# Two of four weight-block sums of a Strassen pair: VectorE adds replaced by accumulating transfers

## The chip, the cores and the metric

The kernel runs on one core of one Trainium2 chip. The metric is the device time of one execution in microseconds (us): 1936.63 us, the median of three runs (1934.05 to 1936.67).

## The reference

A decoder of two layers over 512 tokens with 16 meta tokens in front (528 rows of width 1024, float32). Each layer has a SwiGLU feed-forward block, a token mixer (gated linear attention in layer 0, sliding-window attention in layer 1) and a second feed-forward block, each between two RMS norms. The change touches only the first product of the four feed-forward blocks:

```python
def swiglu(x, w_in, w_out):                       # D_MODEL 1024, D_FF 2816
    gate, up = jnp.split(x @ w_in, 2, axis=-1)
    return (jax.nn.silu(gate) * up) @ w_out
...
    h = h + 0.5 * rmsnorm(swiglu(rmsnorm(h, g[0]), w_ffn_in[layer, 0], w_ffn_out[layer, 0]), g[1])
```

## The kernel before, in words

**Precision.** A float32 operand is split into a high part in TensorE's fast float32 format and the rest. A product is three matmuls: high by high, low by high, high by low. Every weight block therefore passes from a raw tile (128x512, 256 KB, loaded by SP) through one copy on ScalarE (ACT, the high part) and one subtraction on VectorE (DVE, the rest) into a `w` tile of two halves.

**The feed-forward block.** The 22 hidden tiles are worked in four chunks, `FF_CHUNKS`. The first chunk (4 tiles) uses plain products. The other three chunks have six hidden tiles each. For each hidden tile the gate block g and the up block u are taken together as one 2x2 block matrix of weights and multiplied with the halves of the activations by a Strassen scheme: seven half-size products instead of eight. That makes 72 such pairs in the kernel (4 blocks, 3 chunks, 6 pairs). After each chunk, `out_steps` multiplies the hidden tiles with `w_out` (tiles named `y`).

**One pair.** The left operands of the seven products are named in `split_pair`: with r11 and r12 the two halves of g, and r21 and r22 the two halves of u, they are 11, 12 and 22 (as loaded) and the sums s1 = r21 + r22, s3 = r11 + r21, s2 = s3 + r22 and s4 = r12 + s2. `Strassen.head` does product 11, `body` does s1, s2, 12 and s3, and `tail` does s4 and 22. The order on TensorE (PE) is 11 of the next pair, s4 and 22 of this pair, then s1, s2, 12, s3 of the next, and so on. Each product is 12 matmuls over 264 columns (256 in layer 1). Seven products are one turn. Between products ACT copies results out of PSUM, because the banks are reused: `t.v` (line 778, after s1), `t.u2` (line 780, after s2), the copy into `d` (line 773, after 11). Product s3 adds onto the bank that the `t.u2` copy reads, so it waits for line 780. The hidden tile is split by lines 802 to 807.

**Order and queues.** The order of the work is planned at build time by `Flow`, a clock that counts PE time; jobs yield the time they expect to pass (2.2 us after a load, `STEP` between parts). Each engine then runs its own queue strictly in order. `part` (lines 245 and 246) is the ACT copy and the DVE subtraction of one block of a pair; line 251 is `add`; lines 226 and 227 do the same for plain units such as `w_out`. `raw_tile` takes the raw tiles in rotation from `RAWS` buffers; the SP load into a buffer waits until the buffer's last reader is done. `CHAINS = 2` pairs may be in splitting at once, and `RING = 10` limits the split blocks that wait for PE. GpSimd (POOL) has no work in these chunks; its own work is sums of squares and norms at the ends of the blocks.

In the trace, tiles of 11, 12 and 22 are named `w`, those of the four sums `w_s`, the bank for s4 of a chunk's last pair `e`, and the raw tiles `raw`.

Of the kernel before, what the change touches and what calls it, by code (L numbers as in the profile page):

```python
# [13 lines left out]
ALU = mybir.AluOpType  # L14
# [15 lines left out]
L1 = [(16, 256), (272, 256)]  # L30
L1W = [(16, 512)]
SLOTS = 32
RAWS = 8
RING = 10
STEP = 1.1
CHAINS = 2

CHAIN = 5
# [85 lines left out]
def trunk_kernel(ctx: ExitStack, tc, a, out):  # L124
    nc = tc.nc
    pe, act, dve, pool, sp = nc.tensor, nc.scalar, nc.vector, nc.gpsimd, nc.sync
    flow = Flow()

    cp = ctx.enter_context(tc.tile_pool(name="cp", bufs=1))
    rp = ctx.enter_context(tc.tile_pool(name="rp", bufs=RAWS))  # L130
    hp = ctx.enter_context(tc.tile_pool(name="hp", bufs=SLOTS))
# [15 lines left out]
    def pair_tile(name, dt=F32R):  # L147
        return hp.tile([P, 2, TOK], dt, tag="pair", name=name)
# [29 lines left out]
    units = []  # L178
# [35 lines left out]
    def slot(i):  # L214

        while live[0] + sum(n for j, n in owed.items() if j < i) >= limit[0]:
            yield room[0]
        live[0] += 1
        owed[i] -= 1

    def raw_tile(name):
        return rp.tile([P, 512], F32, tag="raw", name=name)
# [7 lines left out]
    def split_unit(i, raws):  # L230
        yield 2.2
        for raw, m in raws:
            yield from slot(i)
            split_part(i, raw, m)

    def split_pair(i, raws):


        r11, r12, r21, r22 = raws
        parts, ready = loaded[i]  # L240

        def part(name, src):
            yield from slot(i)
            w = pair_tile(f"w{i}_{name}")
            act.activation(w[:, 0, :512], src, AF.Copy)  # L245
            dve.tensor_tensor(w[:, 1, :512], src, w[:, 0, :512].bitcast(F32), op=ALU.subtract)  # L246
            parts[name].append(w)
            ready[name].finish(flow)

        def add(dst, src):  # L250
            dve.tensor_tensor(dst, dst, src, op=ALU.add)  # L251

        yield 2.2
        yield from part("11", r11)
        add(r11, r21)
        add(r21, r22)
        yield STEP
        yield from part("s1", r21)
        yield STEP
        yield from part("s3", r11)  # L260
        add(r11, r22)
        yield STEP
        yield from part("s2", r11)
        yield STEP
        yield from part("12", r12)
        add(r12, r11)
        yield STEP
        yield from part("s4", r12)
        yield STEP
        yield from part("22", r22)  # L270
        chains[0] -= 1
        prefetch()

    def load_unit():
        i = len(loaded)
        asked[0] += costs[i]
        owed[i] = costs[i]
        if isinstance(units[i], list):
            g, u = units[i]
            chains[0] += 1  # L280
            raws = [raw_tile(f"raw{i}_{k}") for k in range(4)]
            for k in (2, 0, 1, 3):
                sp.dma_start(raws[k], (g, u)[k // 2][:, k % 2 * 512 : (k % 2 + 1) * 512])
                dma_end[0] = max(dma_end[0], flow.clock) + 512 * 1.5e-3
            names = ("11", "12", "22", "s1", "s2", "s3", "s4")
            loaded.append(({k: [] for k in names}, {k: Job(None) for k in names}))
            gen = split_pair(i, raws)
        else:
            n = units[i].shape[-1]
            raws = []  # L290
            for c in range(0, n, 512):
                m = min(512, n - c)
                raws.append((raw_tile(f"raw{i}_{c}"), m))
                sp.dma_start(raws[-1][0][:, :m], units[i][:, c : c + m])
            dma_end[0] = max(dma_end[0], flow.clock) + n * 1.5e-3
            loaded.append([])
            gen = split_unit(i, raws)
        split_jobs.append(flow.spawn(gen, dma_end[0] - flow.clock))

    def prefetch():  # L300
        while len(loaded) < cap[0] and asked[0] + costs[len(loaded)] <= freed[0] + ahead[0]:
            if isinstance(units[len(loaded)], list) and chains[0] == CHAINS:
                break
            load_unit()
# [945 lines left out]
    raws = [[raw_tile(f"raw{i}_{c}") for c in (0, 512)] for i in range(2)]  # L1250
# [17 lines left out]
    x.rjob[0] = flow.spawn(factors(0), 2.0)  # L1268
    dma_end[0] = 1.0
    load_unit()  # L1270
    load_unit()
    load_h(1, 0, 2, 4, 6)
    flow.spawn(second(), SECOND)
# [120 lines left out]
```

## Time and profile before

| what | value |
|---|---|
| median of three runs | 1936.63 us (1934.05 to 1936.67) |
| profiled execution, first to last instruction (span) | 1931.9 us; 4.7 us less than the median run, which has the start and the end around it |
| mean granted TensorE clock | 0.993 |
| busy: PE, weight loads (PEld), DVE, ACT, POOL | 98%, 93%, 74%, 52%, 11% |
| instructions on POOL | 417 |
| loads of `raw` from `w_in` | 352 of 256 KB, median 2.9 us from issue to landing |
| hardware DMA queue | 172.11 MB, 28.5% of the 16 DMA engines |

An engine that is busy for 98% of the span leaves little to gain by relieving others; where it does wait, the chain of waits and the timeline name the engine it waited for. The busy shares are averages over stages, so the twelve chunks are read by themselves in the prediction. The start-to-start distance of neighbouring products on PE shows lost time better than the busy column, because matmuls overlap.

### The profile page before, as it was taken

The numbers are of one execution on the slowest core, as the hardware profiler recorded it, in microseconds if no ns is written. First come the engines' busy times: TensorE is split into PE (matmuls) and PEld (weight loads), VectorE is DVE, ScalarE is ACT, GpSimd is POOL, SyncE is SP. The second block draws the span as 40 slices with busy tenths as digits, with TensorE's granted clock in tenths as the row PEclk, the third lists the DMA queues.
The fourth block names the chain that finished last, engine by engine and source line by source line (L and its number), as shares of the span: only waits on it lengthen the run. The fifth ranks groups of instructions, "written<-read, shape, count | busy, mean of one in ns | idle before, by whom it ended". The sixth has DMA issues, their size and how long they took to land.

```text
span 1931.9 us, 37400 instructions
## 1 busy us (share of the span) xinstructions
PE 1893.9 (98%) x14522; PEld 1803.6 (93%) x14522; DVE 1420.2 (74%) x2868; ACT 1000.5 (52%) x2268; POOL 217.3 (11%) x417
## 2 busy tenths in 40 slices
PE   8999999999999999999999999999998999999997
PEld 8999999999999999999999898989976898989897
DVE  7885858676364788585887786868688779858584
ACT  5662636653245556363674553536645665636363
POOL 2000000311111300000033000000351140000002
PEclk9999999999999999999999999999998999999998
DMA  4332323322113123233351223333321212333331
GB/s 163 109 97 90 104 89 113 107 77 73 38 56 110 56 76 101 93 100 98 101 168 45 66 86 112 91 112 104 122 66 34 74 48 72 97 103 108 102 112 44
DMA packets 102145, 174.63 MB, mean 90 GB/s; under 512 B 11472, under 2 KB 24272, under 8 KB 101968
## 3 DMA queue, kind: packets, MB, share of 16 engines
q1 hardware_dynamic: 101680, 172.11, 28.5%
q8 instruction: 114, 1.87, 0.4%
q14 instruction: 63, 0.52, 0.1%
q10 hardware_dynamic: 288, 0.13, 0.0%
HBM read 170.10 MB, written 2.10 MB: 89 GB/s over the span
## 4 chain that ended last, share of the span: by engine, by line
PE 70%; DVE 19%; ACT 6%; issue 3%; POOL 1%; DMA 0%; SPq 0%; DVEq 0%; ACTq 0%; POOLq 0%
PE y L162 30%; PE x L162 16%; PE a L162 11%; DVE raw L251 5%; PE c L162 4%; DVE w_s L246 4%; DVE w L246 3%; ACT w_s L245 3%; PE d L162 2%; DVE w L227 1%; PE o L162 1%; ACT w L226 1%; PE sc L162 1%; PE po L162 1%; DVE hidl0f L807 1%
## 5 line engine op out<-in xcount | busy, mean ns | idle before, releaser
L246 DVE TENSOR_TENSOR w_s<-raw,w_s 128x512 fp32r<-128x512 f32 x288 | 194.1, 691 | 129.5 <-ACT w_s L245 127.2
L162 PE MATMUL y<-hidl0f,w 128*128 128x272 f32 (+1 forms) x2112 | 261.0, 285 | 0.0
L227 DVE TENSOR_TENSOR w<-raw,w 128x512 fp32r<-128x512 f32 x378 | 243.8, 672 | 20.7 <-ACT w L226 18.8
L162 PEld LDWEIGHTS y<-hidl0f,w 128*128 128x128 f32 x2112 | 258.9, 188 | 0.2
L245 ACT ACTIVATE w_s<-raw 128x512 fp32r<-128x512 f32 x288 | 175.3, 628 | 149.5 <-DVE raw L251 146.0
L162 PE MATMUL y<-hidl1f,w 128*128 128x512 f32 (+1 forms) x1344 | 249.4, 346 | 0.0
L162 PEld LDWEIGHTS y<-hidl1f,w 128*128 128x128 f32 x1344 | 212.3, 188 | 33.2 <-ACT hidl1f L407 0.3
L226 ACT ACTIVATE w<-raw 128x512 fp32r<-128x512 f32 x378 | 208.6, 587 | 33.9 <-PE y L162 29.2
L403 POOL TENSOR_TENSOR acc_post<-acc_post,sq_post 128x256 f32<-128x256 f32 (+1 forms) x72 | 59.1, 821 | 1383.3 <-ACT sq_post L402 1382.6
L251 DVE TENSOR_TENSOR raw<-raw,raw 128x512 f32<-128x512 f32 x288 | 198.0, 688 | 5.5
L246 DVE TENSOR_TENSOR w<-raw,w 128x512 fp32r<-128x512 f32 x216 | 148.4, 688 | 40.4 <-ACT w L245 39.1
L245 ACT ACTIVATE w<-raw 128x512 fp32r<-128x512 f32 x216 | 133.9, 621 | 47.9 <-PE y L162 47.6
L162 PE MATMUL x<-x_l0m,w 128*128 128x272 f32 (+1 forms) x1200 | 158.4, 289 | 0.0
L162 PEld LDWEIGHTS x<-x_l0m,w 128*128 128x128 f32 x1200 | 149.5, 189 | 1.1
L587 DVE TENSOR_TENSOR Y<-y,Y 128x256 f32<-128x256 f32 (+2 forms) x176 | 82.4, 473 | 73.5 <-PE y L162 73.0
L162 PE MATMUL a<-zl0f_t,w_s 128*128 128x264 f32 x864 | 117.6, 285 | 3.9 <-ACT c L780 3.9
L162 PE MATMUL a<-zl1f_t,w_s 128*128 128x256 f32 x864 | 115.3, 283 | 1.9 <-ACT c L780 1.6
L162 PEld LDWEIGHTS a<-zl0f_t,w_s 128*128 128x128 f32 x864 | 110.0, 188 | 5.2 <-ACT c L780 5.2
L162 PEld LDWEIGHTS a<-zl1f_t,w_s 128*128 128x128 f32 x864 | 107.0, 189 | 4.6 <-ACT c L780 4.5
L162 PE MATMUL x<-x_l0f,w 128*128 128x256 f32 (+1 forms) x768 | 100.8, 292 | 6.1 <-ACT w L226 5.7
L162 PEld LDWEIGHTS x<-x_l0f,w 128*128 128x128 f32 x768 | 97.5, 193 | 7.3 <-ACT w L226 5.9
L162 PE MATMUL x<-x_l1f,w 128*128 128x256 f32 (+1 forms) x576 | 92.8, 320 | 0.0
(485 smaller groups left out, 3318.8 us busy)
## 6 DMA issues: line engine op xcount, KB each, us to landing
raw<-in_w_in SPq DMA_DIRECT2D x352, 256.0 KB, 2.9
raw<-in_w_out SPq DMA_DIRECT2D x96, 256.0 KB, 3.3
raw<-in_gla_in SPq DMA_DIRECT2D x50, 256.0 KB, 3.1
raw<-in_w_last SPq DMA_DIRECT2D x48, 256.0 KB, 3.0
raw<-in_w_out SPq DMA_DIRECT2D x64, 128.0 KB, 2.9
raw<-in_gla_out SPq DMA_DIRECT2D x16, 256.0 KB, 2.8
raw<-in_w_q SPq DMA_DIRECT2D x16, 256.0 KB, 3.6
raw<-in_swa_out SPq DMA_DIRECT2D x16, 256.0 KB, 2.8
```

The costliest lines, as they stand in the source:

```text
L162: inst = pe.matmul(o, lhs, rhs, start=start, stop=stop, skip_group_check=onto)
L226: act.activation(w[:, 0, :m], raw[:, :m], AF.Copy)
L227: dve.tensor_tensor(w[:, 1, :m], raw[:, :m], w[:, 0, :m].bitcast(F32), op=ALU.subtract)
L245: act.activation(w[:, 0, :512], src, AF.Copy)
L246: dve.tensor_tensor(w[:, 1, :512], src, w[:, 0, :512].bitcast(F32), op=ALU.subtract)
L251: dve.tensor_tensor(dst, dst, src, op=ALU.add)
L403: pool.tensor_tensor(sums[0][:, :n], sums[0][:, :n], t[:, :n], op=ALU.add)
L587: dve.tensor_tensor(y, p[:, :n], y, op=ALU.add)
L807: dve.scalar_tensor_tensor(t.hid[:, 1, g], t.h, -1.0, t.hid[:, 0, g].bitcast(F32), op0=ALU.mult, op1=ALU.subtract)
```

## The change

Per pair, five raw tiles are loaded instead of four: r11, r12, r22, and two tiles that become sums, `r1` (loaded with the first half of u) and `r3` (loaded with the first half of g). POOL then issues two transfers from memory that add onto these tiles: the second half of u onto `r1`, which makes s1, and the first half of u onto `r3`, which makes s3. The two other sums stay on DVE: r22 onto `r3` (s2) and s2 onto r12 (s4). The planner's waits change: 2.2 us to the accumulating transfers (`LANDED`, as before), then 11, then 2.5 us (`ADDED`) before s1, and s3 comes one step after s1 as before. There are 11 raw buffers instead of 8, and the scratch for descriptors of POOL's transfers is set to 8192 bytes.

```diff
-RAWS = 8
+RAWS = 11
...
+LANDED = 2.2
+ADDED = 2.5
...
-        r11, r12, r21, r22 = raws
+        r11, r12, r22, r1, r3 = raws
         parts, ready = loaded[i]
+        (g, u), half = units[i], lambda t, c: t[:, c * 512 : (c + 1) * 512]
...
-        def add(dst, src):
-            dve.tensor_tensor(dst, dst, src, op=ALU.add)
-
-        yield 2.2
+        def onto(dst, src):
+            pool.dma_start(dst, src, accum_op=ALU.add)
+
+        yield LANDED
+        onto(r1, half(u, 1))
+        onto(r3, half(u, 0))
         yield from part("11", r11)
-        add(r11, r21)
-        add(r21, r22)
+        yield ADDED
+        yield from part("s1", r1)
         yield STEP
-        yield from part("s1", r21)
+        yield from part("s3", r3)
+        dve.tensor_tensor(r3, r3, r22, op=ALU.add)
         yield STEP
-        yield from part("s3", r11)
-        add(r11, r22)
-        yield STEP
-        yield from part("s2", r11)
+        yield from part("s2", r3)
         yield STEP
         yield from part("12", r12)
-        add(r12, r11)
+        dve.tensor_tensor(r12, r12, r3, op=ALU.add)
...
-            raws = [raw_tile(f"raw{i}_{k}") for k in range(4)]
-            for k in (2, 0, 1, 3):
-                sp.dma_start(raws[k], (g, u)[k // 2][:, k % 2 * 512 : (k % 2 + 1) * 512])
+            raws = [raw_tile(f"raw{i}_{k}") for k in range(5)]
+            for k, src, c in ((0, g, 0), (3, u, 0), (4, g, 0), (2, u, 1), (1, g, 1)):
+                sp.dma_start(raws[k], src[:, c * 512 : (c + 1) * 512])
...
-    nc = bacc.Bacc("TRN2", target_bir_lowering=False, num_devices=1)
+    nc = bacc.Bacc("TRN2", target_bir_lowering=False, num_devices=1, dynamic_dma_scratch_size=8192)
```

Line numbers of the changed kernel are 2 or 3 higher: 778, 780, 782 and 806 become 781, 783, 785 and 809. On DVE 144 additions go, on POOL 144 transfers come (two for each pair, with nothing between those of a chunk), on SP 72 loads come. Outside the twelve chunks the order on PE, ACT and DVE stays as it was, apart from a few matmuls of one `w_out` product.

**PE at the end of the first chunk.** Before: product 12 of the last pair (tile `d`), five matmuls of s4 (`e`), then s3 (`a_1`), then the rest of s4.

```order
L162 MATMUL d_1136<-zl0f_211_946,w_12_1780 128x264 x6
L162 MATMUL e_1897<-zl0f_220_766,w_s_1801 128x264 x5
L162 MATMUL a_1_1133<-zl0f_t_1000,w_s_1735 128x264 x6
L162 MATMUL a_1_1133<-zl0f_t_1017,w_s_1735 128x264 x6
L162 MATMUL e_1897<-zl0f_220_766,w_s_1801 128x264
L162 MATMUL e_1897<-zl0f_221_781,w_s_1801 128x264 x6
```

The same place now:

```order
L164 MATMUL d_1140<-zl0f_210_923,w_12_1815 128x264 x6
L164 MATMUL d_1140<-zl0f_211_945,w_12_1815 128x264 x6
L164 MATMUL a_1_1137<-zl0f_t_1002,w_s_1771 128x264 x6
L164 MATMUL a_1_1137<-zl0f_t_1019,w_s_1771 128x264 x6
L164 MATMUL e_1909<-zl0f_220_766,w_s_1842 128x264 x6
L164 MATMUL e_1909<-zl0f_221_781,w_s_1842 128x264 x6
```

The five matmuls of s4 that stood ahead of s3 now stand behind it.

**ACT at the same place.** From the copy into `d` (after product 11 of the last pair) to the `t.u2` copy (line 780, now 783), which s3 waits for. Before:

```order
L773 ACTIVATE d_1136<-a_1_1133 128x264
L245 ACTIVATE w_s_1757<-raw_0_1606 128x512
L226 ACTIVATE w_1_1777<-raw_512_1651 128x256
L245 ACTIVATE w_12_1780<-raw_1_1607 128x512
L226 ACTIVATE w_0_1798<-raw_0_1689 128x512
L795 ACTIVATE c_1616<-c_1616 128x264
L245 ACTIVATE w_s_1801<-raw_1_1607 128x512
L226 ACTIVATE w_1_1820<-raw_512_1691 128x256
L245 ACTIVATE w_22_1825<-raw_3_1609 128x512
L806 ACTIVATE hidl0f_8_1615<-c_1616 128x528
L778 ACTIVATE c_1750<-c_1_1135 128x264
L226 ACTIVATE w_0_1843<-raw_0_1727 128x512
```

Now:

```order
L776 ACTIVATE d_1140<-a_1_1137 128x264
L248 ACTIVATE w_12_1815<-raw_1_1613 128x512
L228 ACTIVATE w_1_1829<-raw_512_1700 128x256
L798 ACTIVATE c_1624<-c_1624 128x264
L809 ACTIVATE hidl0f_8_1623<-c_1624 128x528
L248 ACTIVATE w_s_1842<-raw_1_1613 128x512
L781 ACTIVATE c_1758<-c_1_1139 128x264
L228 ACTIVATE w_0_1852<-raw_0_1736 128x512
L248 ACTIVATE w_22_1861<-raw_2_1614 128x512
L783 ACTIVATE c_1758<-a_1_1137 128x264
```

Before, the `t.u2` copy follows the last row shown, so eleven instructions stood between the two copies; now eight do, and the hidden tile (line 806, now 809) comes ahead of two splits that it followed.

**ACT in the middle of a chunk**, from the `t.v` copy (line 778, now 781) on. Before:

```order
L778 ACTIVATE c_1486<-c_1_1135 128x264
L245 ACTIVATE w_11_1559<-raw_0_1476 128x512
L780 ACTIVATE c_1486<-a_1_1133 128x264
L782 ACTIVATE c_1486<-d_1136 128x264
L245 ACTIVATE w_s_1577<-raw_2_1478 128x512
L245 ACTIVATE w_s_1593<-raw_0_1476 128x512
```

Now:

```order
L781 ACTIVATE c_1492<-c_1_1139 128x264
L248 ACTIVATE w_22_1572<-raw_2_1350 128x512
L248 ACTIVATE w_11_1577<-raw_0_1480 128x512
L248 ACTIVATE w_s_1606<-raw_3_1483 128x512
L783 ACTIVATE c_1492<-a_1_1137 128x264
L248 ACTIVATE w_s_1634<-raw_4_1484 128x512
L785 ACTIVATE c_1492<-d_1140 128x264
```

Three splits stand between the two copies instead of one; the last of them, s1, reads a tile (`raw_3`) that an accumulating transfer completes.

## The prediction

> **What bounds the kernel now.** I read the page's busy shares first, then a table by stage of the twelve Strassen chunks (the only places where the change moves work), then what TensorE waits for, then the timelines of one place where it waits.
>
> ```profile
> PE 1893.9 (98%) x14522; PEld 1803.6 (93%) x14522; DVE 1420.2 (74%) x2868; ACT 1000.5 (52%) x2268; POOL 217.3 (11%) x417
> L251 DVE TENSOR_TENSOR raw<-raw,raw 128x512 f32<-128x512 f32 x288 | 198.0, 688 | 5.5
> ```
>
> TensorE is busy nearly all the time. The 288 additions of line 251 hold VectorE for 198.0 us, of which the change takes half, 99 us. The columns of the next table are PE, PEld, DVE, ACT and POOL busy, the granted clock, the DMA share and GB/s; the first and the last chunk and the sum of the twelve:
>
> ```profile
> 84.10:148.60 64.50, 63.94 (x523) 63.73 (x522) 52.00 (x94) 37.21 (x80) 0.00 (x0) 1.00 0.35 110
> 1821.70:1883.90 62.20, 61.92 (x521) 61.45 (x520) 51.31 (x92) 38.08 (x81) 0.00 (x0) 1.00 0.33 102
> sum 768.00, PE 762.17 PEld 755.35 DVE 617.13 ACT 451.46 POOL 0.00; mean PE 63.51 PEld 62.95 DVE 51.43 ACT 37.62 POOL 0.00
> ```
>
> In the chunks, 768 us together, PE is busy for 762, DVE for 617 (80%), ACT for 451, and POOL not at all. So the 99 us of DVE are off the path almost everywhere; what can be gained is the little that PE still waits. The waits, with columns total us, times, longest:
>
> ```profile
> PE a L162 <- ACT c L780: 5.5, 12, 0.7
> PEld a L162 <- ACT c L780: 9.7, 19, 1.0
> ACT w_s L245 <- DVE raw L251: 146.0, 169, 2.7
> ```
>
> PE waits 12 times for line 780, the copy of `t.u2`: as many times as there are chunks. ACT, which makes that copy, waits 146 us for the very additions of which half go. One chunk's end on PE:
>
> ```profile
> 137.11 1.64 PE L162 MATMUL c<-zl0f_t,w_s 128*128 128x264 f32 x12
> 138.58 1.61 PE L162 MATMUL a<-zl0f_t,w_s 128*128 128x264 f32 x12
> 140.03 1.63 PE L162 MATMUL d<-zl0f,w 128*128 128x264 f32 x12
> 141.50 0.76 PE L162 MATMUL e<-zl0f,w_s 128*128 128x264 f32 x5
> 142.82 1.72 PE L162 MATMUL a<-zl0f_t,w_s 128*128 128x264 f32 x12 [0.56 <-ACT c L780]
> ```
>
> Products start 1.47 us apart, 0.122 us for each matmul. Five matmuls from 141.50 would end at 142.11; s3 starts at 142.82, so 0.71 us are lost, 0.56 of them shown as idle.
>
> **The additions removed, at a chunk's end.** ACT there, and the DVE work that it waits for:
>
> ```profile
> 139.67 0.62 ACT L245 ACTIVATE w<-raw 128x512 fp32r<-128x512 f32 x1
> 141.05 0.65 ACT L806 ACTIVATE hidl0f<-c 128x528 fp32r<-128x528 f32 x1 [0.76 <-DVE c L803]
> 141.60 0.37 ACT L778 ACTIVATE c<-c 128x264 f32<-128x264 f32 x1
> 141.87 0.62 ACT L226 ACTIVATE w<-raw 128x512 fp32r<-128x512 f32 x1
> 142.39 0.38 ACT L780 ACTIVATE c<-a 128x264 f32<-128x264 f32 x1
> ```
>
> ```profile
> 138.11 0.68 DVE L251 TENSOR_TENSOR raw<-raw,raw 128x512 f32<-128x512 f32 x1
> 138.71 0.68 DVE L227 TENSOR_TENSOR w<-raw,w 128x512 fp32r<-128x512 f32 x1
> 139.31 0.42 DVE L802 TENSOR_TENSOR c<-a,c 128x264 f32<-128x264 f32 x1
> 139.65 0.68 DVE L246 TENSOR_TENSOR w_s<-raw,w_s 128x512 fp32r<-128x512 f32 x1
> 140.25 0.42 DVE L227 TENSOR_TENSOR w<-raw,w 128x256 fp32r<-128x256 f32 x1
> 140.59 0.43 DVE L803 TENSOR_TENSOR c<-c 128x264 f32<-128x264 f32 x1
> ```
>
> The results of s1 and s2 were there when the next products began, 138.58 and 140.03, but ACT copied them only at 141.60 and 142.39, because the hidden tile (line 806) stood ahead of them and waited for line 803, which DVE reached late behind an addition and three subtractions. In the new order line 802's and 803's successors follow each other. Product 22 ends near 137.3; with one 256-wide subtraction (0.36 from start to start, 140.25 to 140.59) and two operations of 0.42 the hidden tile can start on ACT between 138.2 and 138.6. Behind it stand, by the starts above, the hidden tile itself 0.55, a split 0.52, the `t.v` copy 0.27 and two more splits 0.52 each, 2.4 us, then the copy of 0.38: it ends between 141.0 and 141.4. In the new order s3 follows product 12 at once and could start at 141.50. So the wait goes, or a tenth of a microsecond of it stays. What is late next there is nothing that PE needs: the splits of `w_out` that stood between get later by one or two places.
>
> How much that is over all chunks: the PE row gives 5.5 us, the PEld row 9.7 (it holds also seven waits inside chunks). Twelve times the 0.15 us by which the idle of the place above falls short of its loss (0.71 less 0.56) added to 5.5 makes 7.3; I leave 0.07 at each end, 0.8 together, and take 6.5 us. Trainium skill, "Perfetto Trace Analysis", Identifying the Most-Contended Engine: matmul busy time is a bad measure of what is left on TensorE, since matmuls are pipelined, and weight-load time a better one. By that rule the gain would be the PEld row's whole 9.7 us and the time 1926.9.
>
> **The additions removed in the middle of a chunk.** A turn of seven products there:
>
> ```profile
> 128.31 1.62 PE L162 MATMUL a<-zl0f_t,w_s 128*128 128x264 f32 x12
> 129.76 1.66 PE L162 MATMUL d<-zl0f,w 128*128 128x264 f32 x12
> 131.25 1.50 PE L162 MATMUL a<-zl0f_t,w_s 128*128 128x264 f32 x11
> ```
>
> ```profile
> 128.99 0.63 ACT L806 ACTIVATE hidl0f<-c 128x528 fp32r<-128x528 f32 x1
> 129.52 0.37 ACT L778 ACTIVATE c<-c 128x264 f32<-128x264 f32 x1
> 129.79 0.62 ACT L245 ACTIVATE w<-raw 128x512 fp32r<-128x512 f32 x1
> 130.31 0.38 ACT L780 ACTIVATE c<-a 128x264 f32<-128x264 f32 x1
> ```
>
> Here the copy ends at 130.69 and s3 starts at 131.25 without a wait: 0.56 us to spare. From the row of line 795 to this copy three splits stood on ACT, now four, which costs 0.52; in return the hidden tile no longer has two splits and a DVE addition (0.69) ahead of it. I take nothing for it, with a cover of about half a microsecond.
>
> **The accumulating transfers.** Nothing in this trace accumulates in a transfer or is issued by POOL. Nearest rows (columns: KB each, median us from issue to landing), in the window 90 to 140 us and then over the whole run:
>
> ```profile
> raw<-in_w_in SPq DMA_DIRECT2D x11, 256.0 KB, 2.8
> raw<-in_w_out SPq DMA_DIRECT2D x5, 256.0 KB, 3.3
> ```
>
> ```profile
> H<-in_h SPq DMA_DIRECT2D x4, 256.0 KB, 5.6
> ```
>
> I bound one from below by the plain load of the same tile, 2.8 us, and from above by the slowest transfer of that size, 5.6, and take 4.2, the middle, since two operands must be read. The loop in which it stands: the raw tile that becomes s1 is loaded into the buffer that block 22 of two pairs earlier leaves, and ACT's split of that 22 stands one turn and two splits ahead of its split of s1. That is 7 x 1.47 + 2 x 0.52 = 11.3 us, less the split (0.62) and the subtraction (0.69) of 22, less the load of 2.8: 7.2 us remain for the transfer, and with the half microsecond of cover on ACT 7.7 before PE waits. Both bounds fit. The second transfer, s3, is split one copy later; what follows it on ACT, lines 785 and 776, is needed only 4 us later or more. While the first two pairs of a chunk are prepared, in the `w_out` product before it, there is more time still. So I cost the transfers at nothing. POOL, with 0.00 us of work in the chunks, has nobody behind them; SP has 72 more loads, on which no engine waits except through the tiles. A pair moves seven blocks instead of four: the DMA share goes from 0.35 to about 0.6, still short of full. The raw buffers and the scratch have no time of their own.
>
> **Sum.** Nothing but the chunk ends: 6.5 us less. The profiled span of 1931.9 becomes 1925.4; the median of the runs lies 4.7 us above that span, so 1936.6 becomes 1930.1.
>
> **Rivals.** *The gain is eaten at the same place.* Before, five matmuls of s4 (5 x 0.122 = 0.61 us) covered part of the copy's lateness; now none do. If the copy comes only 0.6 us earlier, PE still loses its 0.7. For it: ACT's queue there still holds eight instructions. Against: the walk above gains 1.0 to 1.4 us of the 1.3 needed. Time 1934 to 1939; chance 0.20.
>
> *The copy in the middle of the chunks becomes late.* Two splits more stand between the `t.v` and `t.u2` copies. It decides as soon as the hidden tile on ACT gains less than the 0.52 that the added split costs and the 0.56 of cover is used up. An overshoot of 0.3 us, half a split, in five turns of twelve chunks is 60 x 0.3 = 18 us: with the gain at the ends, 1948. For it: the half-microsecond cover; against: DVE sheds two of four additions a turn. Slower; chance 0.18.
>
> *The accumulating transfer is slow.* Past 7.7 us it holds ACT's queue, and the `t.u2` copy behind the s1 split holds PE, in the two turns of each chunk (fourth pair to fifth, fifth to sixth) in which the loop is tight: 24 times. At 8.4 us (three plain loads) that is 24 x 0.7 = 17 us, 1947; at 11.2 (four) 24 x 3.5 = 84, 2014. For it: the trace has no row for a transfer that POOL issues or that adds, and two operands must be read for each result. Against: both nearest rows lie well below. Chance 0.17. Trainium skill, "SBUF — State Buffer", SBUF: two separate sides: descriptors of POOL-issued transfers are written by GpSimd, which VectorE locks out during some operations, so that a transfer of 620 ns took 3100. It says that this holds for two-port modes, which TENSOR_TENSOR does not have; no row here shows it, since POOL issues nothing.
>
> **How the numbers follow.** My forecast, gains of 4 to 9.7 us, has 0.45. A difference under 0.2% (3.9 us) can hardly be told from none in this kernel. Faster: 0.46, the forecast and a sliver of the mildest rivals; same: 0.19; slower: 0.35, the two slow rivals. The range starts at 1926, just under the whole PEld row (1926.9), and goes to 1956, which takes in the late copies with an overshoot of 0.4 us and the mild end of the slow transfer; its bad end, about 0.1, and what is left below stay out.
>
> **What would show it.** Right: the row PE <- ACT for the `t.u2` copy (line 783) vanishes or falls under 2 us; the waits of ACT for line 251's successors fall by more than half; products in the middle of chunks stay 1.47 us apart; transfers on POOL land in 3 to 6 us. Wrong: line 783 as a releaser of PE many times a chunk (late copies); ACT waiting for a DMA at the s1 split (slow transfer); five-microsecond-long busy spans on POOL.

## The result and the profile after

| | before | after |
|---|---|---|
| median of three runs | 1936.63 us | 1923.77 us (1922.40 to 1925.93) |
| ratio, 95% interval | | 0.9938 [0.9921, 0.9956] |
| profiled execution, span | 1931.9 us | 1920.6 us (its own time 1922.4) |
| ratio of a second comparison, 5 runs against 9 | | 0.9952 [0.9939, 0.9964] |

The change makes the kernel faster, by 12.9 us in the first comparison and 9.3 us (1935.41 to 1926.16) in a second, the first experiment below. The forecast was a gain of 6.5 us.

The busy shares of the profile after:

```profile
PE 1885.4 (98%) x14522; PEld 1798.7 (94%) x14522; DVE 1340.4 (70%) x2724; ACT 993.5 (52%) x2268; POOL 341.4 (18%) x561
```

VectorE is busy for 80 us less (1420.2 to 1340.4), TensorE for 8.5. The prediction took 99 us for the additions by their own row; but back to back an operation of 0.68 us adds only 0.60 to the busy time (138.11 to 138.71 in the prediction's rows), which makes 87 of the 99. The table by stage for the twelve chunks, with the columns of the prediction: the first, the last and the sum.

```profile
84.27:147.85 63.58, 63.58 (x523) 63.58 (x522) 46.08 (x83) 36.54 (x80) 5.26 (x7) 1.00 0.56 154
1810.93:1872.50 61.57, 61.57 (x521) 61.42 (x520) 48.76 (x86) 37.78 (x81) 4.37 (x5) 1.00 0.47 129
sum 758.00, PE 757.28 PEld 753.55 DVE 567.59 ACT 443.81 POOL 61.80; mean PE 63.11 PEld 62.80 DVE 47.30 ACT 36.98 POOL 5.15
```

The chunks take 758.0 us where they took 768.0: 10.0 us less, and in the first one PE and PEld are busy for the whole stretch. The waits that answer to those of before (line 783 was 780; lines 264 and 269 are the two additions that stay):

```profile
PEld a L164 <- ACT c L783: 1.7, 5, 0.4
PE a L164 <- ACT c L783: 0.6, 3, 0.2
ACT w_s L248 <- DVE raw L264: 69.1, 67, 1.8
ACT w_s L248 <- DVE raw L269: 15.2, 11, 1.8
```

PE's wait for the `t.u2` copy is down from 5.5 to 0.6 us, PEld's from 9.7 to 1.7. The end of the first chunk on PE, on ACT and on DVE:

```profile
140.10 1.62 PE L164 MATMUL d<-zl0f,w 128*128 128x264 f32 x12
141.56 1.63 PE L164 MATMUL a<-zl0f_t,w_s 128*128 128x264 f32 x12
143.02 1.16 PE L164 MATMUL e<-zl0f,w_s 128*128 128x264 f32 x8
```

```profile
138.42 0.65 ACT L809 ACTIVATE hidl0f<-c 128x528 fp32r<-128x528 f32 x1 [1.19 <-DVE c L806]
138.97 0.62 ACT L248 ACTIVATE w_s<-raw 128x512 fp32r<-128x512 f32 x1
139.49 0.37 ACT L781 ACTIVATE c<-c 128x264 f32<-128x264 f32 x1
139.76 0.62 ACT L228 ACTIVATE w<-raw 128x512 fp32r<-128x512 f32 x1
140.28 0.62 ACT L248 ACTIVATE w<-raw 128x512 fp32r<-128x512 f32 x1
140.80 0.37 ACT L783 ACTIVATE c<-a 128x264 f32<-128x264 f32 x1
```

```profile
137.28 0.42 DVE L229 TENSOR_TENSOR w<-raw,w 128x256 fp32r<-128x256 f32 x1
137.62 0.42 DVE L805 TENSOR_TENSOR c<-a,c 128x264 f32<-128x264 f32 x1
137.96 0.42 DVE L806 TENSOR_TENSOR c<-c 128x264 f32<-128x264 f32 x1
```

On DVE line 806 now follows line 805 directly; the hidden tile starts on ACT at 138.42 instead of 141.05, the `t.u2` copy is done at 141.17, and s3 starts at 141.56, 1.46 us behind product 12, without a wait.

The loss inside chunks went too. In the first chunk of layer 1's second block, product 12 (`d`), s3 and the next 11, before and then after:

```profile
1677.92 1.57 PE L162 MATMUL d<-zl1f,w 128*128 128x256 f32 x12
1679.61 1.69 PE L162 MATMUL a<-zl1f_t,w_s 128*128 128x256 f32 x12
1681.14 1.57 PE L162 MATMUL a<-zl1f,w 128*128 128x256 f32 x12
```

```profile
1668.49 1.59 PE L164 MATMUL d<-zl1f,w 128*128 128x256 f32 x12
1669.92 1.58 PE L164 MATMUL a<-zl1f_t,w_s 128*128 128x256 f32 x12
1671.34 0.88 PE L164 MATMUL a<-zl1f,w 128*128 128x256 f32 x6
```

Before, s3 came 1.69 us after product 12 and the next product 1.53 us after s3; now 1.43 and 1.42. The timeline puts no idle mark on that place of before: the matmul in front counts as busy until 1679.49, and the 0.12 us left are too short for one. A late copy costs twice: the wait itself, and 0.10 to 0.11 us more between two matmuls of the product behind it, at every one of these places.

I added up these losses over all chunks: every start-to-start distance of two matmuls, less the usual distance of its shape (0.122 us for 264 columns, 0.118 for 256, in both kernels), where the difference is over 0.05 us.

| us lost in twelve chunks | before | after |
|---|---|---|
| at the ends (from s4 of the last pair on, its last products included) | 8.9 | 2.2 |
| inside the chunks | 2.3 | 0.0 |
| all smaller deviations together | 0.6 | -0.2 |

The differences are 6.7, 2.3 and 0.8 us, 9.8 together. The last row hangs on the yardstick: there are over 6000 distances, so 0.001 us more or less in the usual distance moves it by 3 us for each of the two main shapes. The rest of the 12.9 us lies outside the chunks (1.3 us by the spans) and in the step from the profiled runs to the medians. Spans and clocks of the changed kernel in the two comparisons, and the chunks' sum in the second:

```profile
core 0: 1920.6 us, clock 0.995
```

```profile
core 0: 1925.1 us, clock 0.992
sum 758.13, PE 757.39 PEld 753.63 DVE 567.75 ACT 443.85 POOL 62.80; mean PE 63.12 PEld 62.80 DVE 47.31 ACT 36.99 POOL 5.23
```

The same program differs by 4.5 us in its span while its chunks agree within 0.13 us. Runs of the kernel before spread likewise, from 1930.57 us (clock 0.995) to 1936.79 (clock 0.993) in one series of 21. So three runs against three can be off by 3 us, and 9 to 10 us is the better figure for the change.

### The profile page after: what moved, and what is told of

Same layout as the page of the kernel before. It is cut to its first block, busy times and chain, and to the rows that moved or that the text cites. A ratio compares the mean times of both kernels' runs of the same rounds, so it can differ in the third digit from the quotient of the medians.

```text
span 1920.6 us, 37874 instructions
## 1 busy us (share of the span) xinstructions
PE 1885.4 (98%) x14522; PEld 1798.7 (94%) x14522; DVE 1340.4 (70%) x2724; ACT 993.5 (52%) x2268; POOL 341.4 (18%) x561
## 4 chain that ended last, share of the span: by engine, by line
PE 89%; DVE 6%; ACT 2%; POOL 1%; issue 1%; DMA 0%; SPq 0%; DVEq 0%; POOLq 0%; ACTq 0%
PE y L164 31%; PE a L164 21%; PE x L164 16%; PE c L164 9%; PE d L164 5%; PE o L164 1%; DVE w L229 1%; PE e L164 1%; PE po L164 1%; PE sc L164 1%; ACT w L228 1%; PE ps L164 0%; DVE x_l0f L429 0%; PE st_go L164 0%; DVE w_s L249 0%
## 5 line engine op out<-in xcount | busy, mean ns | idle before, releaser
L254 POOL DMA_DIRECT2D raw<-in_w_in x144 | 125.9, 935 | 968.2 <-DMA raw<-in_w_in 443.9
L228 ACT ACTIVATE w<-raw 128x512 fp32r<-128x512 f32 x378 | 207.9, 587 | 35.0 <-PE y L164 26.9
L248 ACT ACTIVATE w<-raw 128x512 fp32r<-128x512 f32 x216 | 130.4, 621 | 47.9 <-PE y L164 47.6
```

What stands on the lines that cost most here:

```text
L228: act.activation(w[:, 0, :m], raw[:, :m], AF.Copy)
L254: pool.dma_start(dst, src, accum_op=ALU.add)
```

## The experiments

Theory A, the prediction's: the gain is VectorE's time, because ScalarE's copies out of PSUM stand in its queue behind work that waits for VectorE. Theory B: the gain comes from what came with the change, more raw buffers and earlier loads. All ratios are to the kernel before, from five rounds.

**The changed kernel again**, no edit.

> The changed kernel once more, in the same call as the three next ones and against the kernel before. Both theories (the gain is VectorE's time ahead of ScalarE's copies out of PSUM; or it comes from elsewhere) are indifferent to this run; it settles the size: 0.9938 with an interval of 0.9921 to 0.9956 so far. If the difference between 12.9 us and the 9.8 us that the twelve chunks account for is the clock of single runs, the ratio with more rounds is 0.994 to 0.996; if it is real, 0.993 to 0.994.

Measured: 1926.16 us, ratio 0.9952 [0.9939, 0.9964]. The gain is 9.3 us, so what the first comparison had beyond the chunks' 10 us did not come again.

**Eleven raw buffers and the small scratch in the kernel before.**

```diff
-RAWS = 8
+RAWS = 11
...
-    nc = bacc.Bacc("TRN2", target_bir_lowering=False, num_devices=1)
+    nc = bacc.Bacc("TRN2", target_bir_lowering=False, num_devices=1, dynamic_dma_scratch_size=8192)
```

> The kernel before with 11 raw buffers and the small descriptor scratch, its four additions on DVE as they were. Theory A (the gain is DVE time taken out of the queue that ACT's PSUM copies wait for): no change, ratio 0.998 to 1.002, and PE still waits 12 times for line 780, 5 to 6 us. Theory B (the gain comes from earlier loads through more buffers): most of the 0.6% is there, ratio below 0.997.

Measured: 1935.52 us, ratio 1.0002 [0.9993, 1.001]. Its wait for the copy stays what it was:

```profile
PE a L162 <- ACT c L780: 5.4, 12, 0.8
```

Theory B falls as far as the number of buffers goes; earlier loads were not tried by themselves, but the run below with two additions put back keeps them and has no gain.

**The kernel before without the two additions.**

```diff
-        add(r11, r21)
-        add(r21, r22)
```

> The kernel before without the two additions that make s1 and s3 (left out, so those blocks are unsummed); no accumulating transfer, 8 raw buffers. Theory A: the whole gain, ratio 0.992 to 0.995, no wait of PE for line 780 worth over 2 us. Theory B: ratio near 1.000.

Measured: 1926.77 us, ratio 0.9958 [0.9945, 0.997], and no row of PE waiting for the `t.u2` copy is left. Leaving out the additions is worth 8.6 us, the whole gain within the two intervals; the transfers that replace them cost nothing that these runs can tell.

Two things keep this from being the time of two additions alone. The queues come out in another order without them: at all twelve ends all of s4 stands behind s3, as the change has it at eight. And the gain does not lie in the same places. By the sum of distances this kernel loses 0.7 us at the ends but 2.5 inside the chunks, all of it in layer 1, where the kernel before loses 2.3 and the changed one nothing. So leaving out the additions heals the ends; what heals the inside in the changed kernel, its order or sums that are ready earlier, stays open.

**Two additions put back into the changed kernel.**

```diff
         yield from part("11", r11)
+        for _ in range(2):
+            dve.tensor_tensor(idle, r11, r11, op=ALU.add)
```

> The changed kernel with two additions of the same size per pair put back on DVE behind block 11 (into a tile that nobody reads); transfers, buffers and the order on PE stay as changed. Theory A: the gain goes, and since PE no longer has matmuls of s4 ahead of s3 as cover, the time is that of before or up to 0.4% longer: ratio 0.998 to 1.004. Theory B: ratio stays at 0.994.

Measured: 1936.8 us, ratio 1.0012 [1.0001, 1.0023]: all of the gain is lost, with transfers, buffers and the order on PE, POOL and SP as in the changed kernel; on ACT and on DVE some twenty instructions changed places. The place of the loss is new. PE's wait for the copy, a row of the waits, and then one of the places, from the timelines of PE and ACT:

```profile
PE a L165 <- ACT c L786: 4.5, 11, 1.1
```

```profile
316.43 1.62 PE L165 MATMUL d<-zl0f,w 128*128 128x264 f32 x12
318.35 1.74 PE L165 MATMUL a<-zl0f_t,w_s 128*128 128x264 f32 x12 [0.29 <-ACT c L786]
```

```profile
315.53 0.65 ACT L812 ACTIVATE hidl0f<-c 128x528 fp32r<-128x528 f32 x1 [0.84 <-DVE c L808]
317.92 0.38 ACT L786 ACTIVATE c<-a 128x264 f32<-128x264 f32 x1
```

This is the middle of a chunk, not its end: 1.92 us between products instead of 1.46, because the hidden tile waits for DVE and the copy behind it ends only at 318.30. By the sum of distances this kernel loses 8.1 us inside chunks and 3.2 at their ends.

The additions put back take more than their own time, though. They often stand ahead of the subtraction of block 11 in VectorE's queue, and there they wait for the load of that block, which no addition of before did for long (5.5 us of idle time ahead of all 288). The row of these waits, and the one ahead of the place shown:

```profile
DVE idle L262 <- DMA raw<-in_w_in: 101.3, 50, 7.3
310.45 0.69 DVE L262 TENSOR_TENSOR idle<-raw 128x512 f32<-128x512 f32 x1 [1.27 <-DMA raw<-in_w_in]
```

Followed back through the waits, 6.8 of the 8.1 us lead to such a wait of 0.7 to 3.5 us. So the run shows that a late VectorE takes the whole gain, whatever makes it late, and by the path that the prediction named; it does not show that the time of two additions would do so. At the ends the kernel loses 3.2 us instead of the 8.9 of before, which points to the new order as the larger part of what the ends gained. With a late VectorE that order would have made the second rival come true.

**One addition put back.**

```diff
         yield from part("11", r11)
+        dve.tensor_tensor(idle, r11, r11, op=ALU.add)
```

> The changed kernel with one VectorE addition of 128x512 per pair put back after the split of 11 (its result is read by nobody), where the kernel with two put back had lost the whole gain (1.0012). If the gain follows VectorE's time in proportion, half of 9.3 us is lost: ratio 0.9975 to 0.998. If it is a cover that is used up only past a threshold (about 0.5 us on ScalarE's path to the copies in the middle of the chunks), one addition costs little: 0.9955 to 0.9965, and the second would have cost nearly all.

Measured: 1930.43 us, ratio 0.9979 [0.997, 0.9988]. The gain shrinks to 4.3 us (1934.72 to 1930.43), where two additions put back left none. The loss is again inside the chunks (3.4 us there, 2.2 at the ends as in the changed kernel), and the distances show 0.24 to 0.41 us lost at one place in eight of the twelve chunks. Ahead of each of these eight places the addition waited 0.6 to 1.1 us for the load of block 11. VectorE ahead of the first of them, here and then in the changed kernel:

```profile
738.69 0.69 DVE L266 TENSOR_TENSOR raw<-raw,raw 128x512 f32<-128x512 f32 x1
740.38 0.69 DVE L261 TENSOR_TENSOR idle<-raw 128x512 f32<-128x512 f32 x1 [1.00 <-DMA raw<-in_w_in]
743.26 0.42 DVE L799 TENSOR_TENSOR c<-c,c 128x264 f32<-128x264 f32 x1
```

```profile
738.78 0.69 DVE L264 TENSOR_TENSOR raw<-raw,raw 128x512 f32<-128x512 f32 x1
742.51 0.43 DVE L797 TENSOR_TENSOR c<-c,c 128x264 f32<-128x264 f32 x1 [0.32 <-PE c L164]
```

From the first row to the last VectorE takes 4.57 us here and 3.73 there. The 0.84 us between them are less than the wait of 1.00, so at this place the addition itself would have found room. How large the cover is against an addition that waits for nothing, and so which reading of the expectation holds, these two runs do not show.

**The two remaining additions left out as well.**

```diff
-        dve.tensor_tensor(r3, r3, r22, op=ALU.add)
...
-        dve.tensor_tensor(r12, r12, r3, op=ALU.add)
```

> The changed kernel without the two additions that are still on VectorE (s2 and s4 are left unsummed): what would be left to gain if these too were made by transfers at no cost. By the distances between matmuls the twelve chunks still lose about 3 us against a steady pace, so at most 3 us: ratio 0.9937 to 0.9952. If VectorE's time counted in proportion, another 9 us would go: 0.9905.

Measured: 1923.6 us, ratio 0.9942 [0.993, 0.9955], and by the distances nothing over 0.05 us is left at the ends or inside. The second pair of additions would be worth some 2 us (1.4 by the distances), less than the two intervals can separate. Most of the gain comes with the first pair.

**The additions on POOL, in the kernel before.**

```diff
-        add(r11, r21)
-        add(r21, r22)
+        pool.tensor_tensor(r11, r11, r21, op=ALU.add)
+        pool.tensor_tensor(r21, r21, r22, op=ALU.add)
```

> The kernel before with the two additions moved from DVE to POOL; no accumulating transfer, 8 buffers. Theory A: DVE is relieved just the same, so ratio 0.992 to 0.997 if POOL's additions (estimate 1.5 us each, from 0.82 us for 128x272) neither hold up ACT nor slow DVE. If POOL's additions delay the splits of s1 and s3 or slow DVE's own, ratio 1.000 to 1.01.

Measured: 2017.91 us, ratio 1.043 [1.0416, 1.0444]. The group of POOL's additions and three waits:

```profile
L255 POOL TENSOR_TENSOR raw<-raw,raw 128x512 f32<-128x512 f32 x72 | 94.3, 1310 | 1051.3 <-DVE w L246 977.9 <-DMA raw<-in_w_in 73.4
```

```profile
ACT w_s L245 <- POOL raw L256: 182.7, 62, 3.5
PE a L162 <- DVE c L784: 34.9, 37, 1.1
PE a L162 <- ACT c L780: 29.9, 49, 1.6
```

An addition takes 1.31 us on POOL against 0.69 on VectorE. (Most of the 977.9 us is POOL with nothing to do.) That is not the whole price: the first one writes over r11 and so has to wait until DVE has subtracted the block 11 from it, the second follows it, and ACT's queue waits at the split of s1 with the copies behind it. Relieving VectorE did not help here, since the sum was not ready ahead of its split. The accumulating transfers write to tiles of their own and can run far ahead.

**The accumulating transfer onto r1 twice.**

```diff
         onto(r1, half(u, 1))
+        onto(r1, half(u, 1))
```

> The changed kernel with the accumulating transfer onto r1 (the one that makes s1) issued twice, one after the other, so the second half of u is added twice and s1 holds another sum. Theory of the prediction (the transfer has 2 to 3 us of cover in the tight turns and more elsewhere): a second transfer of 5.0 us comes 2 to 3 us late in the 24 tight turns, 48 to 72 us, ratio to the kernel before about 1.02 to 1.03. Rival, the cover is used up already (in the one tight turn looked at, the s1 split started on ScalarE in the moment the transfer landed): the whole 5.0 us is lost 24 times, 120 us, ratio 1.055. Rival, the loop is loose, since the planner and the 11 buffers run ahead: ratio 0.995, as without the doubling.

Measured: 1925.38 us, ratio 0.9952 [0.9939, 0.9966]: no change. The transfers did not become shorter (median 5.4 us against 5.0 and, in the repetition, 5.3), and POOL mostly waits for the first before it issues the second; 59 of the 106 waits of the second row, 190 us, are for transfers of POOL's own, the others for plain loads:

```profile
raw<-in_w_in POOLq DMA_DIRECT2D x216, 256.0 KB, 5.4
```

```profile
POOL raw L254 <- DMA raw<-in_w_in: 608.2, 106, 34.3
```

Some five further microseconds per pair cost nothing. Both theories with a tight loop fall; my own reading of a tight turn, on which one of them rested, was wrong, since I had taken the landing of one pair's transfer for that of the pair before.

**The s1 split planned earlier, and one buffer less**, in the changed kernel.

```diff
-ADDED = 2.5
+ADDED = 1.1
```

> The changed kernel with ADDED = 1.1 in place of 2.5: the planner puts the s1 split 1.4 us of its clock earlier in ScalarE's queue, nothing else is edited. If the cover of the transfer is used up, ScalarE now waits for the transfer at that split and the copies behind it come late: up to 1.4 us in the 24 tight turns, 34 us, ratio about 1.01, and a row of ScalarE waiting for a DMA of 20 us or more. If there is cover of 2 us, nothing changes: ratio 0.994 to 0.995.

Measured: 1927.38 us, ratio 0.9961 [0.9948, 0.9973], not told apart from the changed kernel. The shortest time from the landing of a transfer onto `r1` to the split of s1 falls from 6.0 to 1.7 us, and no split of a sum waits for a transfer.

```diff
-RAWS = 11
+RAWS = 10
```

> The changed kernel with 10 raw buffers in place of 11. A pair now takes five buffers, so two pairs take ten. With 11 buffers the base tile of s1 goes into the buffer that block 22 of two pairs earlier leaves; with 10 it takes the buffer of a later reader of that pair. If the loop of buffers is at its edge, the loads start later and ScalarE waits for the transfer: ratio 1.01 or more. If the loop has slack, ratio 0.994 to 0.995.

Measured: 1925.24 us, ratio 0.9952 [0.9939, 0.9964]. Ten buffers do as well as eleven. No version that still makes all the sums can be told apart from the changed kernel as faster.

## Why the prediction was right in kind and too small

**The chunk's end: right.** The walk had the hidden tile on ACT between 138.2 and 138.6 (138.42), the copy done between 141.0 and 141.4 (141.17) and s3 at 141.50 (141.56). For all twelve ends it took 6.5 us; the distances give 8.9 less 2.2, which is 6.7. That the sum comes so near is in part luck: the prediction had 7.3 us lost before and 0.8 left, and both were too small by about 1.5. In fact the six ends of layer 0 lose nothing; in layer 1 four ends, where one matmul of s4 still stands ahead of s3, lose 0.4 to 0.5 each, and two lose 0.2.

**The middle of the chunks: the term that was mis-sized.** The prediction saw that the PEld row "holds also seven waits inside chunks" and costed the middle at nothing, by one place of layer 0 that had 0.56 us to spare. The chunks of layer 1 had no such cover; 2.3 us were lost there before and none after, and deviations under 0.05 us gave 0.8 more. So the chunks gained 9.8 us by the distances where the prediction had 6.5. One place does not stand for sixty turns: the row with the count did. Trainium skill, "Perfetto Trace Analysis", Identifying the Most-Contended Engine: weight-load time tells better than matmul time what is left on TensorE. By that rule the prediction had 9.7 us and 1926.9; the trace agrees in the main, with 10.0 us in the chunks, though the row itself fell by 8.0 (9.7 to 1.7), and the second comparison gave 1926.16.

**What is left of the first comparison: spread.** 12.9 us were measured, of which 11.3 lie between the two profiled spans and 10.0 in the chunks. The 4.7 us that the prediction put around the span of before were mostly spread too. In the series of 21 a run of that kernel is in the median 2.1 us longer than its span, and the profiled run after is 1.8 longer (1922.4 less 1920.6). So the profiled execution of before stood for a run of some 1934.0, near the fastest of its three. Together with the middle of the chunks the spread is why 1923.77 lies under the low end of 1926.0; the repetition, 1926.16, lies just inside it.

**The transfers: nothing, as costed, but by another loop.** I took 4.2 us with bounds of 2.8 and 5.6. The groups of transfers after:

```profile
raw<-in_w_in SPq DMA_DIRECT2D x424, 256.0 KB, 3.8
raw<-in_w_in POOLq DMA_DIRECT2D x144, 256.0 KB, 5.0
```

The median is 5.0; single ones took 3.9 to 7.7, past the upper bound. The plain loads slowed from 2.9 to 3.8, which I had not costed. It is hidden all the same, because the loop was mistaken: the tile for s1 does not wait for block 22 of two pairs earlier. For the last pair of the first chunk, the loads on SP (the first of the four is of the pair before), the issues on POOL, the split of that block 22 and the split of s1:

```profile
109.10 2.23 SPq L286 DMA_DIRECT2D raw<-in_w_in  x4
```

```profile
114.85 1.75 POOL L254 DMA_DIRECT2D raw<-in_w_in  x2 [10.19 <-DVE w L249]
```

```profile
118.68 0.62 ACT L248 ACTIVATE w<-raw 128x512 fp32r<-128x512 f32 x1
130.01 0.62 ACT L248 ACTIVATE w_s<-raw 128x512 fp32r<-128x512 f32 x1
```

The load into `r1` was issued at 110.4, eight microseconds before the split of that block 22, so its buffer was another, and the transfer landed at 119.8: 10 us of cover instead of the 3 that the prediction's window left. The smallest over all 72 pairs is 6.0 us.

**The rivals.** "The gain is eaten at the same place" falls with the ends; the argument against it was summed wrong and too small, since by the walk's own rows the copy ends 1.4 to 1.8 us earlier (142.77 to between 141.0 and 141.4), not 1.0 to 1.4. "The copy in the middle becomes late" did not happen, but it is the path by which the two runs with additions put back lose their time, once a load holds VectorE up. "The accumulating transfer is slow" falls with the doubled transfer. The trap for transfers that POOL issues, for which the prediction named the Trainium skill, "SBUF — State Buffer", did not show: an issue held POOL for 0.85 to 1.18 us.

**The signs.** PE's row fell under 2 us, the products in the middle stayed 1.46 us apart, transfers landed in 5 us, and the DMA share of the chunks is near the 0.6 foreseen (0.51 to 0.59, only 0.47 in the last): as said. ACT's waits for the additions fell from 146.0 to 84.3 us, not by more than half; what counted was which of them stood ahead of a copy.

## What to carry to other kernels

On an engine that is busy 98% of the time, a relief elsewhere is worth what that engine still waits for it, added up over all places: read the weight-load row with its count, short waits in the middle included, and not one place. An engine off the critical path counts through whoever waits for it in an in-order queue; put one dummy operation of the disputed kind back to measure how much cover there is, and look first whether it waits for something that the original did not wait for, as the two such runs here did. Look also whether a sum that is moved still waits for a reader of the old tile: the same additions on POOL did, and the kernel was slower.

## What was not expected of the hardware

- A 256 KB transfer that adds onto its target lands in 5.0 us (median; 5.3 in the repetition), where plain loads beside it take 3.8 (3.7); those loads took 2.9 before, when a pair moved four blocks instead of seven.
- An addition of 128x512 takes 1.31 us on POOL and 0.69 on VectorE.
- The same kernel's time varies by several microseconds from run to run. In the series of 21 the fastest run had the highest granted clock (0.995), and the three at the lowest (0.991) took 1936.29 to 1936.73 us. In the two profiles of the changed kernel the whole difference of 4.5 us lies outside the Strassen chunks, which repeat within 0.13 us at a clock of 1.00.
